# Fixing the issue order of the feed-forward stages of an encoder layer, with the second token chunk walked backwards

## The chip, the cores and the metric

One core of a Trainium2 chip runs the whole kernel. The time is device microseconds for one execution; the median of three runs of the kernel before is 1975.6 us (1968.54 to 1975.73). One further execution was profiled. It took 1982.1 us, of which the trace covers a span of 1980.3 us from the first to the last instruction.

## The reference

One layer of a bidirectional encoder on 1,536 tokens (1,024 of a prompt, 512 of a sample), all in float32, followed by a last RMSNorm:

```python
x = x + mix @ w_out                       # mix: two groups of attention heads, each normalised
hn = rms_norm(x, g_ffn)
x = x + (silu(hn @ w_gate) * (hn @ w_up)) @ w_down
y = rms_norm(x, g_final)
```

The model width is 1,024 and the hidden width (D_FF) 2,816. The change touches only the feed-forward part: gate and up products, the gated product, the down product, and the residual sum after it.

## The kernel before, in words

**Arithmetic.** Every float32 operand is split into a high part and a low part (hi on ScalarE as a copy, lo on VectorE as the difference), and a product is made of three matmuls per tile: hi x hi, hi x lo, lo x hi (mm3, L146). The feed-forward products use a Strassen-Winograd scheme: a 2 x 2 block product is done with seven products instead of eight, and sums of blocks are made before and after. So each operand exists in seven versions: some of the blocks themselves, the others sums or differences.

**Gate and up (gate_up, L1123).** The tokens are handled as two chunks of 768 (ck), the hidden units as 22 slices of 128 (f), so there are 44 steps u. A step makes the seven products in the order SEQ = 1, 6, 2, 7, 5, 4, 3. Each is four mm3 sets of 12 matmuls with 384 columns in a PSUM bank named x (mm), y or z. Between them stands the chain on the results: p1 copies product 1 on ScalarE, u2, u3, c22, c21, c12 are sums on VectorE (L1143 to L1160), sl1 and sl2 are Silu on ScalarE, and t1, t2 are the gated products on VectorE (L1157, L1164). Products 2, 7, 4, 3 accumulate into a bank that already holds another product, so each must wait until that one has been read: product 2 for p1, product 7 for u2, product 4 for u3, product 3 for c22. After every second slice GpSimd makes five sums of the results for the down products (L1175) and writes all seven versions to DRAM (hid_d, L1176). The results stand in a tile named as with two buffers, a12 and a21 with one each.

**Operands of a step.** w_sum (L1043) is a generator that prepares the seven weight versions of the next step, one portion after each product: GpSimd sums (fs, L1061), ScalarE hi (fhi, L1056), VectorE lo (flo, L1057). Its weights come through fw_load (L1031), 512 KB for gate and 512 KB for up, in three buffers named fraw, on the SP queue. h_sum (L983) makes the seven versions of a chunk: a sum where needed (mix, L991), hi (L1006) and lo (L1007), 1,536 columns each. raw_tile (L960) loads one of the six token tiles of a chunk, scales it on VectorE (L969, xh), transposes it with eight TensorE instructions (L210, pt) and copies the two results out on ScalarE and VectorE. The six tiles of chunk 1 are written in the main loop behind slices 5, 7, 9, 11, 13 and 15 (L1271).

**Down (L1314).** 42 products m of 33 matmuls with 512 columns: seven versions n in the order WSEQ = 2, 4, 3, 1, 6, 5, 7, each for six pairs of token tiles b (three of each chunk). The left operand comes back from hid_d (left, L1218, 704 KB, then hi and lo of 1,408 columns). The weights come as quarter tiles of 256 KB (wq, L1195), one or two for a piece, with a GpSimd sum where there are two (L1215), then hi and lo (dhi L1204, dlo L1205); eleven pieces make one version, and there is room for 22. x_back (L1280) reloads x for the residual. The buffers of this stage reuse the room of the gate and up stage, and a tile waits for the old tiles that it lies on.

**What sets the order.** The text gives every instruction its engine, and within one engine the framework's scheduler orders instructions by its own model of their times and their place in the text. So instructions of a later step can stand ahead of an earlier one's on a queue; matmuls of product 1 or 6 of slice u + 1 are found between those of slice u, and the left operands of the first down products were converted near 1330 us. SP's and GpSimd's DMA queues are ordered in the same way.

Of the kernel before, what the change touches and what calls it, by code (L numbers as in the profile page):

```python
# [8 lines left out]
F32 = mybir.dt.float32  # L9
# [47 lines left out]
def hymba_layer_kernel(  # L57
# [725 lines left out]
    def out_pre(i):  # L783
# [3 lines left out]
        o = room("qa", "o_in") if i < NO else late.tile([P, D], F32, tag="o_in", name="o_in", bufs=3)  # L787
# [172 lines left out]
    def raw_tile(ck, b, pool, tag, bufs, banks):  # L960
# [18 lines left out]
        transposed_whole(xh, put, banks)  # L979

    hpool, hsum = {}, {}

    def h_sum(n, eng=nc.gpsimd):  # L983

# [9 lines left out]
        if n == 1:  # L994
            src = b11
            if eng is nc.vector:
                mix(b12, b22, b12, ALU.subtract)
# [22 lines left out]
    steps = [(ck, f) for ck in range(2) for f in range(NFF)]  # L1020
    turn = dict(fs=0, fhi=0, flo=0)
# [9 lines left out]
    def fw_load(u, old=False):  # L1031
        if u < len(steps):
# [10 lines left out]
    def w_sum(u):  # L1043

        if u >= len(steps):
            while True:
                yield
# [3 lines left out]
        def temp():  # L1051
            return turned("fs", F32, 2, 2)
# [16 lines left out]
        parts(6, s2)  # L1069
        yield  # L1070
        parts(2, a12)
        if u == 0:
            yield
            g, up = wraw.pop(u)
            a11, a12, a21, a22 = g[:, :4], g[:, 4:], up[:, :4], up[:, 4:]
        s3 = temp()
        add(s3, a11, a21, ALU.subtract)
        if u > 0:
            yield
        parts(7, s3)  # L1080
        s4 = temp()
        add(s4, a12, s2, ALU.subtract)
        yield
        parts(5, s1)
        yield
        parts(4, a22)
# [34 lines left out]
    sums, a12, a21 = {}, {}, {}  # L1121

    def gate_up(u, extra=None):  # L1123
        ck, f = steps[u]
        j, odd = divmod(f, 2)
        if not odd:
            sums[ck, j] = fp.tile([P, 7, HC], F32, tag="as", name="as", bufs=2)
# [6 lines left out]
        for n in SEQ:  # L1134
            acc = {1: x, 2: x, 6: y, 7: y, 4: y, 5: z, 3: z}[n]
            (wh, wl), (hh, hl) = wsum.pop((u, n)), hsum[n]
# [28 lines left out]
            next(nxt)  # L1165
            if extra:
                extra(n)
        if not odd:
            a21[0] = t2
            return  # L1170

        A11, A12, A21, A22 = part[3], t1, a21[0], part[4]
        for n, p, q, op in ((5, A11, A12, ALU.add), (6, A21, A11, ALU.subtract), (2, A21, A22, ALU.add),
                            (1, A11, A22, ALU.add), (7, A12, A22, ALU.subtract)):
            nc.gpsimd.tensor_tensor(out=part[n], in0=p, in1=q, op=op)  # L1175
        nc.gpsimd.dma_start(out=hid_d[ck][:, :, j], in_=a.rearrange("p n (c t) -> p (n c) t", t=P))  # L1176
# [7 lines left out]
    down = [(n, b) for n in WSEQ for b in range(NB)]  # L1184
    PA, PB = 9, 13
    made = dict(piece=0, left=0)
# [20 lines left out]

    def piece(n, j):
        p, *q = quads(n, j)
        src = dpool["b"].tile([P, 512], F32, tag="wq", name="wq", bufs=6)  # L1210
# [223 lines left out]
```

## Time and profile before

| | |
|---|---|
| median of 3 runs | 1975.6 us |
| profiled execution | 1982.1 us |
| its span | 1980.3 us |
| TensorE (PE) busy | 1847.2 us, 93% |
| weight loads (PEld) busy | 1543.9 us, 78% |
| VectorE (DVE) busy | 1345.5 us, 68% |
| ScalarE (ACT) busy | 915.8 us, 46% |
| GpSimd (POOL) busy | 850.3 us, 43% |
| granted TensorE clock, mean | 0.962 |

A busy engine is one with an instruction running; matmuls overlap, so TensorE's share says only when it had something to do. The times between its instructions, and what ended them, tell more. In windows of the trace each column gives busy time and the number of instructions of an engine, then the granted TensorE clock as a part of full speed, the busy share of the 16 DMA engines and their rate.

### The profile page before, as it was taken

What the parts mean: (1) busy time and instruction counts of PE and PEld (TensorE: products, weight loads), DVE (VectorE), ACT (ScalarE), POOL (GpSimd) and SP (SyncE); (2) the same over time, 40 slices, a digit from 0 to 9 for tenths busy, and PEclk for the clock granted to TensorE, in tenths of its full rate; (3) what the DMA queues carried; (4) which work ended last, traced back from release to release, by engine and by line L of the source; (5) the groups of instructions that cost most, each with busy time, mean ns of one, the idle gap of its engine ahead of it and who ended that gap; (6) DMA issues with size and microseconds to landing.
All of it is one profiled execution on the core that took longest, in us unless ns stands there. A gap on an engine that the chain in (4) does not pass through costs nothing.

```text
span 1980.3 us, 27660 instructions
## 1 busy us (share of the span) xinstructions
PE 1847.2 (93%) x9682; PEld 1543.9 (78%) x9682; DVE 1345.5 (68%) x2554; ACT 915.8 (46%) x1667; POOL 850.3 (43%) x688
## 2 busy tenths in 40 slices
PE   6999999999899998799899999979999997999998
PEld 4666666667566666588899999979999995887886
DVE  7566756757656667565977677877767765756765
ACT  5465666656565566343433343433433332324431
POOL 3323333344355442100666566666567543642110
PEclk9999999999999898899999999989999998999999
DMA  7799899997898799443353343433443448866652
GB/s 261 139 178 165 169 180 157 179 153 148 162 166 171 160 218 191 157 154 113 107 147 124 110 124 103 120 100 105 118 131 103 133 126 323 271 219 215 222 174 94
DMA packets 421692, 316.26 MB, mean 160 GB/s; under 512 B 262336, under 2 KB 365904, under 8 KB 421552
## 3 DMA queue, kind: packets, MB, share of 16 engines
q1 hardware_dynamic: 398928, 229.93, 48.2%
q0 software_dynamic: 22624, 84.56, 15.3%
q8 instruction: 76, 1.25, 0.3%
q14 instruction: 64, 0.52, 0.1%
HBM read 202.71 MB, written 51.41 MB: 128 GB/s over the span
## 4 chain that ended last, share of the span: by engine, by line
PE 72%; DMA 13%; DVE 7%; issue 3%; ACT 2%; POOL 2%; SPq 1%; DVEq 0%; ACTq 0%; POOLq 0%
PE acc L155 36%; PE yacc L155 11%; PE mmacc L155 7%; PE zacc L155 7%; DMA pT<-p 6%; PE sc L687 4%; PE pv L755 3%; PE sc L686 2%; DVE flo L1057 2%; DMA left<-hid_d 1%; DMA hid_d<-as 1%; DMA vna<-va 1%; DMA wq<-in_w_down_dram 1%; DMA fraw<-in_w_up_dram 1%; PE pt L210 1%
## 5 line engine op out<-in xcount | busy, mean ns | idle before, releaser
L155 PE MATMUL acc<-dhi,left 128*128 128x512 f32 x924 | 291.2, 396 | 16.4 <-ACT left L1231 13.1
L155 PE MATMUL acc<-hth,whi 128*128 128x512 f32 x576 | 243.6, 423 | 1.6 <-ACT hth L285 1.5
L155 PE MATMUL acc<-htl,whi 128*128 128x512 f32 x576 | 240.9, 418 | 2.9 <-DVE htl L288 2.7
L155 PE MATMUL acc<-hth,wlo 128*128 128x512 f32 x576 | 240.5, 418 | 0.0
L1057 DVE TENSOR_TENSOR flo<-fs,fhi 128x512 fp32r<-128x512 f32 x176 | 173.3, 987 | 86.7 <-ACT fhi L1056 83.5
L155 PEld LDWEIGHTS acc<-dhi,left 128*128 128x128 f32 x924 | 175.0, 190 | 57.6 <-ACT left L1231 13.9
L1056 ACT ACTIVATE fhi<-fs 128x512 fp32r<-128x512 f32 x176 | 109.3, 628 | 190.1 <-POOL fs L1061 78.5
L125 POOL TENSOR_TENSOR wlo<-wraw,whi 128x1024 fp32r<-128x1024 f32 x48 | 117.8, 2456 | 182.7 <-ACT whi L124 158.9
L740 DVE SCALAR_TENSOR_TENSOR p<-t,p 128x768 f16<-128x768 f32 (+3 forms) x192 | 145.5, 765 | 72.4 <-ACT p L736 71.6
L734 ACT ACTIVATE t<-t,mt 128x768 f32<-128x768 f32 (+3 forms) x192 | 137.5, 716 | 122.2 <-DVE mt L727 119.6
L155 PE MATMUL acc<-dlo,left 128*128 128x512 f32 x462 | 182.3, 395 | 0.0
L1061 POOL TENSOR_TENSOR fs<-fraw 128x512 f32<-128x512 f32 x88 | 130.8, 1502 | 84.0 <-DMA fraw<-in_w_up_dram 74.8
L1057 DVE TENSOR_TENSOR flo<-fraw,fhi 128x512 fp32r<-128x512 f32 x132 | 165.7, 1255 | 1.3 <-ACT fhi L1056 1.3
L1215 POOL TENSOR_TENSOR wq<-wq 128x512 f32<-128x512 f32 x55 | 93.4, 1709 | 158.1 <-DMA wq<-in_w_down_dram 134.5
L736 ACT ACTIVATE p<-t 128x768 f16<-128x768 f32 (+3 forms) x192 | 118.1, 624 | 77.4 <-DMA pT<-p 48.7
L155 PEld LDWEIGHTS acc<-hth,whi 128*128 128x128 f32 x576 | 113.1, 196 | 35.2 <-issue 9.6
L155 PEld LDWEIGHTS acc<-htl,whi 128*128 128x128 f32 x576 | 113.0, 196 | 34.0 <-issue 6.5
L155 PEld LDWEIGHTS acc<-hth,wlo 128*128 128x128 f32 x576 | 113.1, 196 | 30.3 <-issue 6.8
L1056 ACT ACTIVATE fhi<-fraw 128x512 fp32r<-128x512 f32 x132 | 83.0, 629 | 116.3 <-PE yacc L155 93.5
L1232 DVE TENSOR_TENSOR left<-left,left 128x1408 fp32r<-128x1408 f32 x42 | 74.2, 1768 | 89.9 <-ACT left L1231 89.9
L755 PEld LDWEIGHTS <-pT 128*128 128x128 f16 x1536 | 72.7, 99 | 70.8 <-DMA pT<-p 38.1
L1175 POOL TENSOR_TENSOR as<-a,as 128x384 f32<-128x384 f32 x66 | 87.5, 1326 | 94.0 <-DVE a L1164 74.6
(210 smaller groups left out, 4755.8 us busy)
## 6 DMA issues: line engine op xcount, KB each, us to landing
wq<-in_w_down_dram SPq DMA_DIRECT2D x132, 256.0 KB
hid_d<-as POOLq DMA_DIRECT2D x22, 1344.0 KB, 8.0
left<-hid_d SPq DMA_DIRECT2D x42, 704.0 KB
wraw<-in_w_in_dram POOLq DMA_DIRECT2D x46, 512.0 KB, 5.9
fraw<-in_w_gate_dram SPq DMA_DIRECT2D x45, 512.0 KB
fraw<-in_w_up_dram SPq DMA_DIRECT2D x45, 512.0 KB
tabb<-in_tabb_dram POOLq DMA_DIRECT2D x8, 800.0 KB, 6.6
xh<-x_d SPq DMA_DIRECT2D x12, 512.0 KB
```

The costliest lines, as they stand in the source:

```text
L125: eng.tensor_tensor(out=lo, in0=src, in1=hi.bitcast(F32), op=ALU.subtract))
L155: latest[0] = nc.tensor.matmul(out=out, lhsT=a, rhs=b, start=first and i == 0, stop=i == last, skip_group_check=not first)
L687: nc.tensor.matmul(out=out, lhsT=qh[hs, qs], rhs=lx, start=False, stop=True)
L734: nc.scalar.activation(t, t, AF.Exp, bias=mt, scale=-1.0, accum_out=k.den)
L736: nc.scalar.activation(k.p16[:, 0], t, AF.Copy, scale=16384.0)
L740: nc.vector.scalar_tensor_tensor(out=k.p16[:, 1], in0=k.t, scalar=16384.0, in1=k.p16[:, 0], op0=ALU.mult, op1=ALU.subtract)
L755: nc.tensor.matmul(start=j + i == 0, stop=j + i == m, **one)
L1056: nc.scalar.activation(hi, src, AF.Copy)
L1057: nc.vector.tensor_tensor(out=lo, in0=src, in1=hi.bitcast(F32), op=ALU.subtract)
L1061: nc.gpsimd.tensor_tensor(out=o, in0=a, in1=b, op=op)
L1175: nc.gpsimd.tensor_tensor(out=part[n], in0=p, in1=q, op=op)
L1215: nc.gpsimd.tensor_tensor(out=src, in0=src, in1=other, op=q[1])
```

## The change

- From the opening of the feed-forward stage to the end of the kernel, all five engines (TensorE, ScalarE, VectorE, GpSimd and SP, the DMA queues with them) issue their instructions in the order of the text. What the text has ahead of it is ordered as before.
- Chunk 1 takes its slices from 21 down to 0. Slice 22 (the first of chunk 1) therefore uses the weights that slice 21 has just used; they are neither loaded nor split again.
- The five GpSimd sums after a pair of slices, and their write, are put in a list (todo) and issued one after each product of the next slice.
- The opening makes the chunk sums 7, 5, 4, 3 inside slice 0, on VectorE. The first step's weights aren't loaded a second time but for a quarter of up (256 KB). GpSimd's difference of two chunk blocks stands behind a chunk's last input tile.
- In the down stage, the first six products are versions 2 and 4 of chunk 0, the next six those of chunk 1. Loads of quarters and left operands are written ahead of their use (piece_load, left_load), the conversions later. x comes back one pair per place.
- Buffers: four fs in one pool instead of two in each of two, seven wq instead of six, two o_in instead of three.

```diff
-        o = room("qa", "o_in") if i < NO else late.tile([P, D], F32, tag="o_in", name="o_in", bufs=3)
+        o = room("qa", "o_in") if i < NO else late.tile([P, D], F32, tag="o_in", name="o_in", bufs=2)
...
         transposed_whole(xh, put, banks)
+        if b == CT - 1:
+            nc.gpsimd.tensor_tensor(out=raw[0, 1], in0=raw[1, 1], in1=raw[0, 1], op=ALU.subtract)
...
-    steps = [(ck, f) for ck in range(2) for f in range(NFF)]
+    steps = [(0, f) for f in range(NFF)] + [(1, f) for f in reversed(range(NFF))]
...
-        if u < len(steps):
+        if u < len(steps) and u != NFF:
...
-        if u >= len(steps):
+        if u >= len(steps) or u == NFF:
             while True:
                 yield
...
         parts(6, s2)
+        s3 = temp()
+        add(s3, a11, a21, ALU.subtract)
         yield
         parts(2, a12)
...
         s4 = temp()
         add(s4, a12, s2, ALU.subtract)
         yield
+        parts(7, s3)
+        yield
         parts(5, s1)
         yield
-        parts(4, a22)
+        parts(4, wraw.pop(-1) if u == 0 else a22)
         parts(3, s4)
...
-            (wh, wl), (hh, hl) = wsum.pop((u, n)), hsum[n]
+            (wh, wl), (hh, hl) = wsum[u - (u == NFF), n], hsum[n]
...
-            next(nxt)
             if extra:
                 extra(n)
+            next(nxt)
+            if todo:
+                todo.pop(0)()
...
+        def add(n, p, q, op):
+            todo.append(lambda: nc.gpsimd.tensor_tensor(out=part[n], in0=p, in1=q, op=op))
...
-    down = [(n, b) for n in WSEQ for b in range(NB)]
+    down = [(n, b) for ck in range(2) for n in WSEQ[:2] for b in range(ck * HT, ck * HT + HT)]
+    down += [(n, b) for n in WSEQ[2:] for b in range(NB)]
...
     def ahead(n):
 
         if n == 1:
-            left(0)
-            left(1)
+            left_load(0)
+            left_load(1)
...
+            left(0)
         elif n in (7, 5):
             for j in ((2, 3) if n == 7 else (4, 5)):
                 piece_parts(2, j, early[j])
+        elif n == 4:
+            left(1)
...
+    mine = {mybir.EngineType.Activation, mybir.EngineType.DVE, mybir.EngineType.PE, mybir.EngineType.Pool,
+            mybir.EngineType.SP}
+    ctx.enter_context(tc.manual_schedule(engines=mine))
+    t = fB[0].tile([P, NK, P], F32, tag="fraw", name="fraw", bufs=3)
+    wraw[-1] = t[:, 4:]
+    nc.sync.dma_start(out=wraw[-1], in_=w_up[4 * P:, :P].rearrange("(k p) f -> p k f", p=P))
     fw_load(1)
+    def opening_sums(n):
+
+        m = {1: 7, 6: 5, 2: 4, 7: 3}.get(n)
+        if m:
+            h_sum(m, nc.vector)
+            if m != 4:
+                next(first)
+
     for u, (ck, f) in enumerate(steps):
         extra = None
-        if f == NFF - 1:
-            extra = ahead if ck else h_sum
...
+        if u == 0:
+            extra = opening_sums
+        elif u == NFF - 1:
+            extra = lambda n: h_sum(n, nc.vector)
+        elif u == len(steps) - 1:
+            extra = ahead
+            fA.release()
         gate_up(u, extra)
         if ck == 0 and f >= 5 and f % 2 and f // 2 - 2 < CT:
             raw_tile(1, f // 2 - 2, fp, "xh", 1, "dn")
...
+    while todo:
+        todo.pop(0)()
+    for j in range(6, NP):
+        piece_load(2, j)
+    left_load(2)
+    x_back(0)
+    left_load(3)
     for j in range(6, NP):
         piece(2, j)
-    x_back(0)
-    left(2)
-    for b in range(1, NB):
-        x_back(b)
-    left(3)
+    x_back(1)
...
+    slices = {}
+    todo += [(4, j) for j in range(NP)]
+    for m in range(3):
+        slices[m] = [todo.pop(0) for _ in range((4, 4, 3)[m])]
+    for w in range(2, len(WSEQ)):
+        first, n = (6 * w - 3, 3) if w == 2 else (6 * w - 6, 6)
+        for b in range(n):
+            slices[first + b] = [(WSEQ[w], j) for j in range(NP * b // n, NP * (b + 1) // n)]
+    for p in slices[0][:3]:
+        piece_load(*p)
...
         if m:
-            left(m + 3)
...
+            left_load(m + 3)
+        if m == 0:
+            x_back(2)
+        elif m in (3, 4, 5):
+            x_back(m)
+        for p in slices.get(m, ()):
+            if p not in quarter:
+                piece_load(*p)
+        left(m + 2)
+        for p in slices.get(m, ()):
+            piece(*p)
+        for p in slices.get(m + 1, ())[:2]:
+            piece_load(*p)
```

## Rows read from the trace of the kernel before

**Rows 1.** Windows by stage: busy time and instructions of each engine, clock, DMA share, rate.
```profile
0.00:934.00 934.00, 854.08 (x4555) 617.25 (x4556) 605.83 (x1559) 531.29 (x1043) 316.88 (x321) 0.95 0.82 170
934.00:1636.00 702.00, 673.81 (x3762) 667.75 (x3761) 519.52 (x654) 270.97 (x464) 434.34 (x308) 0.97 0.40 118
1636.00:1972.00 336.00, 319.27 (x1369) 258.91 (x1367) 216.45 (x328) 112.84 (x158) 99.09 (x59) 0.97 0.63 220
```

**Rows 2.** Windows without a stop: gate and up stage, down stage.
```profile
1345.00:1620.00 275.00, 274.99 (x1573) 274.66 (x1572) 195.32 (x261) 104.59 (x185) 176.09 (x131) 1.00 0.41 119
...
1800.00:1960.00 160.00, 160.00 (x699) 131.04 (x698) 112.22 (x211) 58.88 (x90) 24.83 (x15) 1.00 0.55 189
```

**Rows 3.** Windows over the places where TensorE stops.
```profile
936.20:962.00 25.80, 18.35 (x85) 17.08 (x84) 24.70 (x29) 15.94 (x22) 12.59 (x7) 0.87 0.37 119
...
1089.00:1104.00 15.00, 11.09 (x52) 10.77 (x50) 11.63 (x11) 3.78 (x8) 10.01 (x6) 0.77 0.39 110
1273.00:1306.00 33.00, 23.21 (x92) 21.75 (x91) 32.57 (x23) 13.22 (x18) 25.54 (x12) 0.74 0.26 74
1329.00:1345.00 16.00, 9.35 (x41) 9.02 (x40) 9.46 (x13) 6.53 (x10) 4.98 (x4) 0.79 0.38 126
1636.00:1676.00 40.00, 26.85 (x105) 20.70 (x104) 18.52 (x20) 10.76 (x14) 10.80 (x7) 0.83 0.88 331
1776.00:1794.00 18.00, 14.77 (x55) 11.03 (x54) 9.86 (x12) 6.79 (x9) 2.10 (x1) 0.91 0.35 137
```

**Rows 4.** Windows of one stop and of the matmuls behind it.
```profile
1287.90:1292.00 4.10, 0.17 (x1) 0.00 (x0) 4.10 (x4) 0.63 (x1) 4.10 (x3) 0.88 0.00 0
1292.00:1296.10 4.10, 4.02 (x13) 4.02 (x14) 4.10 (x3) 0.03 (x1) 4.10 (x2) 0.50 0.02 4
```

**Rows 5.** Instructions by line: ns shortest/median/longest, first and last start, shape.
```profile
L1160 DVE TENSOR_TENSOR c<-zacc,u x44: 543/546/558, 968.6 to 1636.2; 128x384 f32<-128x384 f32 x44
...
L1162 ACT ACTIVATE sl<-c x44: 508/526/528, 969.2 to 1636.9; 128x384 f32<-128x384 f32 x44
...
L1164 DVE TENSOR_TENSOR as<-c,sl x22: 541/543/1645, 985.5 to 1637.4; 128x384 f32<-128x384 f32 x22
...
L1057 DVE TENSOR_TENSOR flo<-fs,fhi x176: 673/693/2094, 825.1 to 1619.8; 128x512 fp32r<-128x512 f32 x176
L1057 DVE TENSOR_TENSOR flo<-fraw,fhi x132: 674/1251/6778, 821.1 to 1616.6; 128x512 fp32r<-128x512 f32 x132
...
L969 DVE SCALAR_TENSOR_TENSOR xh<-xh,rs,g_f x12: 1272/1284/2322, 832.8 to 1080.6; 128x1024 f32<-128x1024 f32 x12
```

**Rows 6.** Instructions by line: the chunk sums, lo, hi and mix.
```profile
L1007 DVE TENSOR_TENSOR h4l<-q,h4h x2: 1746/1750/1753, 939.6 to 1303.7; 128x1536 fp32r<-128x1536 f32 x2
...
L1006 ACT ACTIVATE h4h<-q x2: 1466/1466/1467, 937.8 to 1296.6; 128x1536 fp32r<-128x1536 f32 x2
...
L991 DVE TENSOR_TENSOR q<-q,q x4: 1752/1754/1759, 900.6 to 941.3; 128x1536 f32<-128x1536 f32 x4
```

**Rows 7.** Instructions by line on GpSimd: chunk difference, weight sums, result sums.
```profile
L1267 POOL TENSOR_TENSOR q<-q,q x1: 3647/3647/3647, 1088.5 to 1088.5; 128x1536 f32<-128x1536 f32 x1
...
L1061 POOL TENSOR_TENSOR fs<-fs,fraw x44: 1254/1450/2807, 823.1 to 1605.4; 128x512 f32<-128x512 f32 x44
...
L1175 POOL TENSOR_TENSOR as<-a,as x66: 1002/1398/1993, 973.1 to 1640.9; 128x384 f32<-128x384 f32 x66
```

**Rows 8.** The chain of waits from 1326 to 1346 us: start, us, what.
```profile
1329.33 4.33 DMA left<-hid_d
```

**Rows 9.** The chain of waits from 1640 to 1680 us.
```profile
1642.77 7.73 DMA hid_d<-as
...
1651.01 4.39 DMA x<-x_d
...
1655.42 10.68 DMA left<-hid_d
```

**Rows 10.** Window with the highest DMA rate in the down stage.
```profile
1660.00:1670.00 10.00, 2.00 (x4) 1.19 (x5) 1.62 (x1) 1.38 (x1) 2.31 (x1) 0.50 1.03 406
```

**Rows 11.** The chain of waits from 1770 to 1800 us.
```profile
1779.42 6.02 DMA left<-hid_d
```

More of the change, by code (lines that the diff above doesn't have):

```diff
@@ L1119, in half @@
         return fp.tile([P, HC], F32, tag=tag, name=tag, bufs=bufs)
-    sums, a12, a21 = {}, {}, {}
+    sums, a12, a21, todo = {}, {}, {}, []
     def gate_up(u, extra=None):
@@ L1125, in gate_up @@
         j, odd = divmod(f, 2)
-        if not odd:
+        if (ck, j) not in sums:
             sums[ck, j] = fp.tile([P, 7, HC], F32, tag="as", name="as", bufs=2)
@@ L1164, in gate_up @@
                 v.tensor_tensor(out=t2, in0=c22, in1=sl2, op=ALU.mult)
-            next(nxt)
             if extra:
                 extra(n)
-        if not odd:
-            a21[0] = t2
-            return
[L1172 to L1176, printed above, removed]
+            next(nxt)
+            if todo:
+                todo.pop(0)()
+        if odd:
+            a12[ck, j] = t1
+        else:
+            a21[ck, j] = t2
+        if not ((ck, j) in a12 and (ck, j) in a21):
+            return
+        A11, A12, A21, A22 = part[3], a12[ck, j], a21[ck, j], part[4]
+        def add(n, p, q, op):
+            todo.append(lambda: nc.gpsimd.tensor_tensor(out=part[n], in0=p, in1=q, op=op))
+        add(5, A11, A12, ALU.add)
+        add(6, A21, A11, ALU.subtract)
+        add(2, A21, A22, ALU.add)
+        add(1, A11, A22, ALU.add)
+        add(7, A12, A22, ALU.subtract)
+        todo.append(lambda: nc.gpsimd.dma_start(out=hid_d[ck][:, :, j], in_=a.rearrange("p n (c t) -> p (n c) t", t=P)))
     NB = 2 * HT
     WSEQ = (2, 4, 3, 1, 6, 5, 7)
-    down = [(n, b) for n in WSEQ for b in range(NB)]
+    down = [(n, b) for ck in range(2) for n in WSEQ[:2] for b in range(ck * HT, ck * HT + HT)]
+    down += [(n, b) for n in WSEQ[2:] for b in range(NB)]
     PA, PB = 9, 13
-    made = dict(piece=0, left=0)
+    made = dict(piece=0)
     pieces, lefts, dpool = {}, {}, {}
@@ L1222, in left @@
         ck, c = divmod(b, HT)
[L1223 to L1224 removed]
+        slot = m % 4
         if slot < 2:
@@ L1227, in left @@
         else:
-            hi, lo = (dpool["b"].tile([P, NP, P], F32R, tag=f"left{i}", name=f"left{i}", bufs=2) for i in range(2))
-        raw_lo = lo.bitcast(F32)
-        nc.sync.dma_start(out=raw_lo, in_=hid_d[ck][:, (n - 1) * HT + c])
-        nc.scalar.activation(hi, raw_lo, AF.Copy)
-        nc.vector.tensor_tensor(out=lo, in0=raw_lo, in1=hi.bitcast(F32), op=ALU.subtract)
-        lefts[n, b] = (hi, lo)
+            hi, lo = (dl.tile([P, NP, P], F32R, tag=f"left{i}", name=f"left{i}", bufs=2) for i in range(2))
+        nc.sync.dma_start(out=lo.bitcast(F32), in_=hid_d[ck][:, (n - 1) * HT + c])
+        lefts[m] = (hi, lo)
+    def left(m):
+        if m < len(down):
+            hi, lo = lefts[m]
+            nc.scalar.activation(hi, lo.bitcast(F32), AF.Copy)
+            nc.vector.tensor_tensor(out=lo, in0=lo.bitcast(F32), in1=hi.bitcast(F32), op=ALU.subtract)
     early = []
```

52 lines of the change are left out of this document (14 added, 38 removed).

## The prediction

> **What bounds the kernel now.** I read the windows by stage first: the attention and output part up to 934 us, the gate and up products to 1636 us, the down products to 1972 us [rows 1]. The change touches the last two, and there TensorE is nearly always busy, so the question is what keeps it waiting. A quiet stretch gives the pace [rows 2]: 1573 matmuls in 275 us are 0.1748 us each, so a product of 12 takes 2.1 us and a slice of 84 takes 14.7 us. In the down stage 699 in 160 us are 0.2289 us each, 7.55 us for a product of 33. Next I laid windows over every place where TensorE stops [rows 3] and took from each the matmuls in it at that pace. Lost are: at the opening 25.8 - 85 x 0.1748 = 11 us; round 1089 us 6; at the change of chunk 17; round 1329 us 9; at the start of the down products 40 - 105 x 0.2289 = 16; round 1776 us 5. That is 64 us in all, and no order of the queues can win more than this. Part of it is no idle time: after the stop of 4.1 us the granted clock was 0.50, the 1.2 GHz level, and 13 matmuls took 4.1 us instead of 2.3 [rows 4]. A stop of four microseconds costs six.
>
> **What the change does to each place.** All five queues now run in the order of the text. An instruction that waits holds up everything written behind it on its engine. I go through the places where that order puts a late instruction ahead of an urgent one. Slices are counted 0 to 43, times from the first matmul of the slice.
>
> *The six input tiles of chunk 1, which the diff does not touch.* After slices 5, 7, ... 15, raw_tile scales a tile on VectorE and TensorE transposes it. Now these transposes stand between the third product of that slice and the first of the next. VectorE reaches the scaling only after what the slice's last product releases. In order that is c12, then sl2 on ScalarE, t2, the two splits 4 and 3 for the next slice, and the scaling itself. By the medians of [rows 5] this is 0.55 + 0.53 + 0.54 + 1.25 + 0.69 + 1.28 = 4.8 us, by the minima 4.2; contention with GpSimd may make it 5.5. TensorE has nothing else to do in that time, and then runs slowly, 4.1 - 13 x 0.1748 = 1.8 us by [rows 4]. So 6 x 6.6 = **40 us added** (36 to 46). Before, these transposes lay between matmuls of other groups: the last tile was scaled at 1080.6 us [rows 5], and of the six stretches only the opening holds any. The DMA of the tile is not what is late: it is issued in mid-slice, behind a weight load.
>
> *Opening.* Slice 0 now makes the chunk sums 7, 5, 4, 3, the rest of its own weight sums and those of slice 1. VectorE's queue up to u3 holds lo7, flo7, flo1, u2, mix5, lo5, flo5, mix4, lo4, flo6: five of 1.75 us [rows 6], four splits of about 1 us and one of 0.55, 13.3 us. It starts at 4.1 us (2.1 for the matmuls, 0.5 for p1 as for sl2, 1.5 for h7h) and waits 1.5 us twice for ScalarE after a mix. So u3 is done near 20.9, lo3 and flo4 near 23.6, and product 4 starts there instead of at 10.5. With the slow clock the slice loses about 14.5 us against 11 before: **+3.5** (-3 to +8). The smaller reload (256 KB instead of 1 MB) is worth nothing while VectorE is last; without that cover it is worth at most the 11 us.
>
> *Round 1089 us.* GpSimd's 3.65 us subtraction of the chunk's operands [rows 7] ran here, and a VectorE split beside it took 6.78 us, the maximum in [rows 5]. It moves behind the last input tile, where no PSUM result waits at first. I keep 1 of the 6 us: **-5** (-6 to 0). The Trainium skill ("SBUF — State Buffer", section "Who interferes with whom") says that VectorE instructions with two SBUF inputs and GpSimd instructions reading SBUF take turns on one port for their full length; the trace agrees here. What that would make of the rest is a rival below.
>
> *Change of chunk.* Slice 22 reuses the weights of slice 21: two loads, 7 splits on ScalarE and VectorE and 4 sums go. In slice 21 VectorE has, up to c12, six lo and three mixes of 1.75 us and six results of 0.55, 19.1 us, and waits three times 1.5 us behind a mix. From 4.1 us on that ends at 27.7. Behind it on ScalarE stand sl2, h3h (1.47) and only then p1 of slice 22, done at 30.2. Product 2 of slice 22, due at 14.7 + 4.2 = 18.9, waits 11.3 us, with the slow clock 13: **-4** against 17 (-9 to +2).
>
> *Round 1329 us.* The left operand of the first down product was converted 300 us early; ScalarE stood waiting 4.33 us for its DMA, with p1 and the PSUM chain behind it [rows 8]. Now it is loaded ahead and converted in slice 43. There u3 stands behind it, a stop of about 1.5 us: **-7.5** (-9 to -4).
>
> *Start of the down products.* Before, an x load on SP waited for the 7.73 us write of the last sums, and the left operand behind it landed late, after 10.68 us [rows 9]. Now the first six products read chunk 0 alone, and the last write is covered by 45 us of them. What is late next: pieces 9 and 10 lie on the room of a21 and a12 (dlo starts 14 + 22 + 48 + 26 = 110 KB into its pool, a12 at 110.5 KB), which GpSimd's last additions read. These end four times 1.4 us after t2 [rows 7], about 8 us after slice 43; piece 9 is due at 6.2 us. With the conversions TensorE stands about 3 us. Then all eleven pieces of sum 4 are wanted by the fourth product, not the seventh. Up to there SP asks for 5 + 22 quarters (7.1 MB), four left operands (2.9), six x tiles (3.1) and the gains (0.5), 13.6 MB. At the most that the trace shows, 406 GB/s with the DMA engines full [rows 10], that is 33.6 us; with the last sum and split (1.4 + 0.6 + 1.25) 36.9. There are 34.6: three products, 6.9 us of the fourth, the stop of 3, and 2 us in which loads start early. So it is 2 us late at that rate and 10 at the 331 GB/s of the stretch before [rows 3]. I take 5 us and the slow clock, with the first stop 10 in all against 16: **-6** (-12 to +6). The third set of pieces has again only three products, for 7.9 MB with fewer others: **+3** (0 to 8).
>
> *Round 1776 us.* Left operands landed late there, one after 6.02 us [rows 11], with quarters ahead of them on SP. Loads now precede the pieces of each product: **-5** (-5 to 0).
>
> *Between these places.* After the last product of a slice VectorE owes t2 and three splits before u2. By the chain above that is 1.6 + 1.25 + 0.69 + 1.25 + 0.55 = 5.3 us, due at 6.3. The cover is 1 us. In the 21 slices with additions on GpSimd it may be gone by 0.2 us: **+4** (0 to 12). The product groups, o_in with two buffers and the write order change nothing that TensorE waits for.
>
> **Sum.** 40 + 3.5 - 5 - 4 - 7.5 - 6 + 3 - 5 + 4 = +23 us. The profiled execution took 1982.1 us (span 1980.3), 6.5 us above the median of 1975.6. From 1982.1 it gives 2005, at the median's level 1998. A measurement here can tell about 0.5% (10 us) from no change.
>
> **Rivals.**
> *The tiles cost nothing; faster.* If VectorE came to the scaling before the slice's last product ended, the 40 us fall away: 1998 - 40 = 1958. It decides as soon as the scaling stands ahead of c12 in VectorE's queue. For it: all other places together give -17. Against it: raw_tile is called after gate_up, and the PSUM chain is written inside. Chance 0.15.
> *A draw.* The order binds less than I think on some engine, or the two crowded slices do better: opening -3, chunk -9, down start -12, no stops between, tiles 37. That sums to 37 - 3 - 5 - 9 - 7.5 - 12 + 0 - 5 + 0 = -5, between 1971 and 1985. Or the change does not hold TensorE to the text; then groups of slice u + 1 still appear within slice u and the time stays near 1976. Chance 0.15.
> *The port shared by VectorE and GpSimd.* In a slice with additions GpSimd needs at least 4 x 1.25 + 5 x 1.0 us [rows 7] and VectorE 7 x 0.67 + 2 x 0.54 [rows 5]. If they always took turns, that is 15.8 us against 14.7. With a fixed order 1.1 us could be lost 21 times, 23 us instead of 4: 2017. This is the rule of the skill's page named above, carried through. Against it: over 275 us with the same work TensorE was always busy [rows 2], as the following slice has room. Chance 0.12.
>
> **How the numbers follow.** The forecast itself has 0.58, and 1980 to 2015 as its own range. With the port rival, slower has 0.70; same 0.15; faster 0.15. The range of 1964 to 2028 takes in the draw, the port rival and the upper bounds of tiles and down start; it leaves out the faster rival and a rest above.
>
> **What would show it.** Right: after each of slices 5, 7, ... 15 a stop of 4 to 6 us before pt on TensorE, released by xh on VectorE, and a slow clock behind it; one long stop at product 4 of slice 0 and one at product 2 of slice 22; none at 1329 us; in the down stage a short stop in the first product and one at the fourth. Wrong: no wait of pt for xh, or stops of over half a microsecond in most slices. If the tiles cost 40 us and the sum still fails, the two crowded slices or the DMA term were mis-sized.

## The result and the profile after

The kernel after takes 2047.8 us in the median of 4 runs (2041.8 to 2052.4), the kernel before 1974.7 us beside it; the ratio is 1.0375, with a 95% interval of 1.0338 to 1.0412. The profiled execution took 2045.0 us. So the change makes the kernel slower, as forecast, but by 63 us from profile to profile where +23 stood, and outside the range. (From median to median it is 73 us: the profiled execution of before lay 7 us above its median, that of after 3 us below. What follows explains the 63.)

The windows by stage answer to [rows 1]. Columns are as there.

```profile
0.00:932.00 932.00, 853.25 (x4552) 616.42 (x4553) 606.73 (x1557) 532.24 (x1043) 322.92 (x324) 0.95 0.83 170
932.00:1697.00 765.00, 683.69 (x3746) 672.50 (x3745) 516.22 (x651) 247.24 (x457) 424.51 (x297) 0.95 0.35 104
1697.00:2035.00 338.00, 325.74 (x1388) 262.91 (x1386) 205.88 (x329) 112.30 (x158) 87.46 (x62) 0.97 0.65 225
```

The loss is in the second row. To compare it with before I take the gate and up stage from the last output-projection matmul to the first down matmul. Before, the two stages overlap: 936.0 to the last gate or up matmul at 1636.2 is 700.2 us; less 20 down matmuls inside it (4.6) and plus 12 of product 6 ahead of it (2.1) this is 698 us. After, it is 765.1: **67 us more**. The down stage gave back some.

TensorE's waits, costliest first, name the two causes: six waits of the tiles' transposes for xh, and 17 short ones of product 7 for u2 (columns: who waited, for whom, us in total, times, longest).

```profile
PE pt L210 <- DVE xh L969: 42.4, 6, 7.6
...
PE yacc L155 <- DVE u L1137: 21.8, 17, 2.0
...
PE mmacc L155 <- ACT p L1134: 6.4, 1, 6.4
PE acc L155 <- ACT left L1245: 5.5, 1, 5.5
```

The third wait, for p1, came to 9.8 us in four places before. Before, no product waited for u2 in this stage (three waits of product 4 for u3 came to 11.0 us), and no transpose of these tiles waited. The windows over the single places answer to [rows 3]: the opening, the old place of the 1089 us stop, the change of chunk, the start of the down products, and round 1776 us.

```profile
932.00:961.00 29.00, 20.58 (x87) 18.43 (x86) 21.87 (x31) 13.81 (x18) 8.15 (x6) 0.76 0.17 54
1333.00:1369.00 36.00, 26.40 (x130) 25.44 (x129) 27.23 (x24) 12.94 (x15) 15.19 (x10) 0.86 0.09 26
...
1697.00:1745.00 48.00, 35.88 (x134) 26.32 (x133) 24.61 (x28) 15.75 (x22) 24.51 (x18) 0.86 0.95 347
1776.00:1794.00 18.00, 18.00 (x80) 14.65 (x79) 7.57 (x9) 4.02 (x5) 5.14 (x4) 1.00 0.70 230
1089.00:1104.00 15.00, 15.00 (x85) 15.00 (x85) 6.53 (x11) 3.87 (x8) 2.67 (x3) 0.97 0.44 128
```

At the pace of [rows 2] the first loses 29.0 - 87 x 0.1748 = 13.8 us (14.5 forecast), the second 13.3 (13 forecast), the third 48.0 - 134 x 0.2289 = 17.3 (10 forecast), the last two nothing. The last two show the same times as before, not the same work, but the old stops are not elsewhere either: the 6.4 us at the change of chunk are the only wait for p1, and the last wait of the down products ends at 1743.4 us. So the crowded slices were sized right as a whole. What was not is seen in VectorE's timeline at the first tile stop (start, us, instruction, the idle time before it and what ended it), where product 3 has just ended and TensorE stands until 1045.4:

```profile
1037.88 0.56 DVE L1154 TENSOR_TENSOR c<-zacc,u 128x384 f32<-128x384 f32 x1 [0.36 <-PE zacc L155]
1039.09 0.94 DVE L1158 TENSOR_TENSOR as<-c,sl 128x384 f32<-128x384 f32 x1 [0.65 <-ACT sl L1156]
1039.95 1.75 DVE L1056 TENSOR_TENSOR flo<-fraw,fhi 128x512 fp32r<-128x512 f32 x1
1041.62 1.48 DVE L1056 TENSOR_TENSOR flo<-fs,fhi 128x512 fp32r<-128x512 f32 x1
1043.02 2.28 DVE L969 SCALAR_TENSOR_TENSOR xh<-xh,rs,g_f 128x1024 f32<-128x1024 f32 x1
```

The instructions and their order are the ones forecast: c12, the wait for sl2, t2, two splits, the scaling. But the scaling takes 2.28 us, close to the maximum in [rows 5] (2.32), not its median of 1.28; the splits 1.75 and 1.48 us. At the sixth tile the same chain looks like this:

```profile
1240.02 0.56 DVE L1154 TENSOR_TENSOR c<-zacc,u 128x384 f32<-128x384 f32 x1 [0.33 <-PE zacc L155]
1241.23 0.56 DVE L1158 TENSOR_TENSOR as<-c,sl 128x384 f32<-128x384 f32 x1 [0.65 <-ACT sl L1156]
1241.75 0.69 DVE L1056 TENSOR_TENSOR flo<-fraw,fhi 128x512 fp32r<-128x512 f32 x1
1242.36 0.68 DVE L1056 TENSOR_TENSOR flo<-fs,fhi 128x512 fp32r<-128x512 f32 x1
1242.96 1.28 DVE L969 SCALAR_TENSOR_TENSOR xh<-xh,rs,g_f 128x1024 f32<-128x1024 f32 x1
```

It is 3 us shorter. What differs is GpSimd. In the window of the first stop it is busy for all of 7.50 us (fifth pair of numbers), in that of the sixth, the last one, for none:

```profile
1037.90:1045.40 7.50, 0.00 (x0) 0.00 (x0) 6.75 (x5) 1.56 (x3) 7.50 (x6) 0.78 0.24 70
1045.40:1052.40 7.00, 6.96 (x34) 6.99 (x35) 1.39 (x3) 1.61 (x3) 5.28 (x5) 0.74 0.12 34
...
1244.30:1250.30 6.00, 5.91 (x22) 5.95 (x23) 0.69 (x1) 0.64 (x2) 3.10 (x1) 0.50 0.22 67
1240.00:1244.40 4.40, 0.01 (x1) 0.04 (x1) 3.57 (x5) 1.56 (x3) 0.00 (x0) 0.90 0.13 38
```

These are the additions that it makes in the first stop:

```profile
1038.61 1.00 POOL L1174 TENSOR_TENSOR as<-as,a 128x384 f32<-128x384 f32 x1
1039.56 1.58 POOL L1060 TENSOR_TENSOR fs<-fs,fraw 128x512 f32<-128x512 f32 x1
1041.11 1.44 POOL L1174 TENSOR_TENSOR as<-a,as 128x384 f32<-128x384 f32 x1
1042.51 1.71 POOL L1060 TENSOR_TENSOR fs<-fraw 128x512 f32<-128x512 f32 x1
1044.18 1.97 POOL L1174 TENSOR_TENSOR as<-a,as 128x384 f32<-128x384 f32 x1
```

Read with VectorE's lines above, they show the two engines taking turns. The addition of 1039.56 ends at 1041.14, and the split of 1039.95 ends 0.56 us later, at 1041.70. The addition of 1041.11 ends at 1042.55, the split of 1041.62 at 1043.10, again 0.55 us later. The next addition ends at 1044.22, and the scaling at 1045.30. A split takes 0.68 us alone, so nearly all of it runs after the addition has ended; what the trace gives as its length is mostly the wait. So each of VectorE's instructions here waits out one of GpSimd's: against the sixth tile that is 0.38 + 1.06 + 0.80 + 1.00 = 3.2 us, the whole of the difference.

GpSimd's timeline in a slice with result sums (here at 1385 us, where product 7 waits for u2) shows what it does: sums of weights (L1060) and of results (L1174) one behind the other without a break, from before the slice's end until after u2.

```profile
1387.08 1.01 POOL L1174 TENSOR_TENSOR as<-as,a 128x384 f32<-128x384 f32 x1
1388.05 1.61 POOL L1060 TENSOR_TENSOR fs<-fs,fraw 128x512 f32<-128x512 f32 x1
1389.62 1.47 POOL L1174 TENSOR_TENSOR as<-a,as 128x384 f32<-128x384 f32 x1
1391.04 1.73 POOL L1060 TENSOR_TENSOR fs<-fraw 128x512 f32<-128x512 f32 x1
1392.73 1.46 POOL L1174 TENSOR_TENSOR as<-a,as 128x384 f32<-128x384 f32 x1
```

VectorE's four instructions in front of u2 there take 0.97, 1.78, 1.49 and 1.77 us. In the next slice, without result sums, the three splits take 0.68 each and u2 is in time.

### The profile page after: what moved, and what is told of

The parts are those of the page before. It is cut to its first block, busy times and chain, and to the rows that moved or that the text cites. A ratio compares the mean times of both kernels' runs of the same rounds, so it can differ in the third digit from the quotient of the medians.

```text
span 2043.3 us, 27575 instructions
## 1 busy us (share of the span) xinstructions
PE 1862.7 (91%) x9682; PEld 1551.8 (76%) x9682; DVE 1332.7 (65%) x2549; ACT 892.5 (44%) x1660; POOL 834.9 (41%) x682
## 3 DMA queue, kind: packets, MB, share of 16 engines
q8 instruction: 76, 1.25, 0.3%
## 4 chain that ended last, share of the span: by engine, by line
PE 68%; DVE 9%; DMA 8%; issue 3%; ACT 2%; POOL 1%; SPq 1%; DVEq 0%; ACTq 0%; POOLq 0%
PE acc L155 33%; PE yacc L155 12%; PE zacc L155 8%; PE mmacc L155 6%; DMA pT<-p 6%; DVE flo L1056 4%; PE sc L687 3%; PE pv L755 3%; PE sc L686 2%; DMA wq<-in_w_down_dram 1%; PE pt L210 1%; DMA vna<-va 1%; DVE c L1154 1%; DVE xh L969 1%; ACT sl L1156 1%
## 5 line engine op out<-in xcount | busy, mean ns | idle before, releaser
L1060 POOL TENSOR_TENSOR fs<-fraw 128x512 f32<-128x512 f32 x85 | 129.8, 1527 | 236.3 <-DMA fraw<-in_w_up_dram 150.7
L1056 DVE TENSOR_TENSOR flo<-fs,fhi 128x512 fp32r<-128x512 f32 x172 | 160.8, 935 | 50.1 <-ACT fhi L1055 50.1
L1226 POOL TENSOR_TENSOR wq<-wq 128x512 f32<-128x512 f32 x55 | 78.3, 1426 | 200.8 <-DMA wq<-in_w_down_dram 200.2
L1156 ACT ACTIVATE sl<-c 128x384 f32<-128x384 f32 x44 | 23.1, 525 | 289.4 <-DVE c L1154 289.4
L1056 DVE TENSOR_TENSOR flo<-fraw,fhi 128x512 fp32r<-128x512 f32 x129 | 130.9, 1015 | 24.3 <-ACT fhi L1055 24.3
L1055 ACT ACTIVATE fhi<-fs 128x512 fp32r<-128x512 f32 x172 | 104.6, 621 | 26.5 <-PE yacc L155 23.8
L687 PE MATMUL sc<-kb,qa 64*128 64x512 f32 (+2 forms) x256 | 114.4, 449 | 0.0
L686 PE MATMUL sc<-ka,qa 128*128 128x512 f32 (+2 forms) x256 | 100.7, 395 | 8.4 <-DVE mt L727 8.3
```

The source lines that it names most:

```text
L686: nc.tensor.matmul(out=out, lhsT=qh[:, qs], rhs=kx, start=True, stop=False)
L687: nc.tensor.matmul(out=out, lhsT=qh[hs, qs], rhs=lx, start=False, stop=True)
L1055: nc.scalar.activation(hi, src, AF.Copy)
L1056: nc.vector.tensor_tensor(out=lo, in0=src, in1=hi.bitcast(F32), op=ALU.subtract)
L1060: nc.gpsimd.tensor_tensor(out=o, in0=a, in1=b, op=op)
L1226: nc.gpsimd.tensor_tensor(out=src, in0=src, in1=other[0], op=quads(n, j)[2])
```

## The experiments

**Theory A**: the excess comes from GpSimd's run of additions, which the fixed order puts beside VectorE's chain at the slice's end. The rivals stand in the expectations. All kernels are edits of the one after. The part ahead of the change, the same in all, took between 924 and 952 us in the profiled executions, so kernels are compared by the length of the gate and up stage, as above. Each length comes from one execution; the down stage, whose text is the same in all, took 337 to 342 us, so differences under some 5 us may be scatter. A whole time without a ratio is one run. The medians of the kernel before, run beside them, were 1982.1 us for 1 to 4, 1983.9 for 5 to 8 and 1981.0 for 9 to 11.

| kernel | edit | stage, us | whole, us | ratio to before (95%) |
|---|---|---|---|---|
| before | | 698 | | |
| after | | 765.1 | 2047.8 | 1.0375 (1.0338 to 1.0412) |
| 1 | zeros written, no result sums | 737.8 | 2020.1 | |
| 2 | result sums on VectorE | 754.7 | 2050.5 | |
| 3 | tiles early | 707.2 | 2010.8 | |
| 4 | 2 and 3 | 715.5 | 1994.1 | 1.0069 (1.0038 to 1.0099) |
| 5 | result sums on GpSimd, in mid-slice | 740.9 | 2024.8 | |
| 6 | 5 and 3 | 701.5 | 1985.3 | 1.0001 (0.9970 to 1.0032) |
| 7 | 3, sums on VectorE behind u2 | 748.8 | 2032.0 | |
| 8 | chunk 1 forward | 772.2 | 2061.6 | |
| 9 | t2 behind the next u2 | 745.0 | 2031.3 | |
| 10 | 6 and 9 | 688.6 | 1969.6 | 0.9946 (0.9912 to 0.9981) |
| 11 | 10, chunk sums in order of need | 685.2 | 1967.0 | 0.9923 (0.9895 to 0.9951) |

**1. No result sums.** The five sums are left out; GpSimd writes zeros in their place.

```diff
-            todo.append(lambda: nc.gpsimd.tensor_tensor(out=part[n], in0=p, in1=q, op=op))
+            todo.append(lambda: nc.gpsimd.memset(part[n], 0.0))
```

> The five sums that GpSimd makes after a pair of slices are left out: it writes zeros in their place, an instruction that reads nothing from SBUF. Everything else, and the order, stays. Theory A (VectorE's instructions with two SBUF inputs are held up by GpSimd's run of ten such instructions, which the new order puts beside the chain at the slice's end): the splits in that chain fall from 1.5-1.8 us to about 0.7, the 17 stops before product 7 (u2, 1.3 us each) go, five tile stops fall from 7.6 us to between 4.4 and 6.5; 2045 becomes about 2012 (2003 to 2022). Theory B (the order of VectorE's queue alone makes these stops, whatever GpSimd does): the stops stay at 1.3 and 7.6 us, the time within 8 us of 2045.

Stage -27 us, and the whole, 2020.1 us, is inside theory A's range. The waits:

```profile
PE pt L210 <- DVE xh L969: 36.8, 6, 6.5
...
PE yacc L155 <- DVE u L1137: 1.6, 2, 1.4
```

All u2 stops but two are gone, without anything taken off VectorE. The tile stops keep 6.5 us, since the sums of weights still stand beside the splits; with GpSimd idle the sixth has 4.4.

**2. The sums on VectorE**, at the same places.

```diff
-            todo.append(lambda: nc.gpsimd.tensor_tensor(out=part[n], in0=p, in1=q, op=op))
+            todo.append(lambda: nc.vector.tensor_tensor(out=part[n], in0=p, in1=q, op=op))
```

> The same five sums are made on VectorE, at the same places of the text; nothing is left out. Theory A: GpSimd's run is gone, so the splits at the slice's end take about 0.7 us and the stops before product 7 go, although VectorE has 0.55 us more ahead of u2; tile stops 4.4 to 6.5 us; about 2015 (2003 to 2025). Theory B: VectorE's queue ahead of u2 and of the tiles only gets longer: stops of 1.3 + 0.6 us and more, about 2060 (2050 to 2075).

Theory A's time was missed: the stage gains 10 us, and 17 stops by u2 stay, 21.2 us. The whole, 2050.5, falls into theory B's range, but the part ahead took 15 us more here than in the kernel after, and the stops did not grow as theory B had it. VectorE's timeline shows why they stay:

```profile
1391.51 1.37 DVE L1158 TENSOR_TENSOR a<-c,sl 128x384 f32<-128x384 f32 x1 [0.65 <-ACT sl L1156]
1392.81 1.78 DVE L1056 TENSOR_TENSOR flo<-fraw,fhi 128x512 fp32r<-128x512 f32 x1
1394.51 0.68 DVE L1056 TENSOR_TENSOR flo<-fs,fhi 128x512 fp32r<-128x512 f32 x1
1395.12 0.68 DVE L1056 TENSOR_TENSOR flo<-fraw,fhi 128x512 fp32r<-128x512 f32 x1
1395.72 1.63 DVE L1174 TENSOR_TENSOR as<-as,a 128x384 f32<-128x384 f32 x1
1397.27 0.54 DVE L1137 TENSOR_TENSOR u<-yacc,p 128x384 f32<-128x384 f32 x1
```

Two splits are short now, but the first result sum stands in front of u2 and takes 1.63 us beside a sum of weights, where the later ones take 0.54.

**3. Tiles early.** The tile is loaded one slice earlier and scaled behind product 7 instead of at the slice's end; the transposes stay where they are.

```diff
+        elif ck == 0 and f >= 5 and f % 2 and f // 2 - 2 < CT:
+            extra = lambda n, b=f // 2 - 2: tile_scale(1, b) if n == 7 else None
         gate_up(u, extra)
+        if ck == 0 and f >= 4 and f % 2 == 0 and f // 2 - 2 < CT:
+            tile_load(1, f // 2 - 2, fp, "xh", 1)
```

> GpSimd's sums as in the changed kernel. Only the six input tiles of chunk 1: their load is written one slice earlier, and the scaling on VectorE stands behind u3 in the middle of slices 5, 7, ... 15; the transposes stay where they are. Both theories: no wait of the transposes for the scaling, 42 us of idle time and some 15 us of slow clock go, less about 1 us for each scaling in mid-slice: 2045 becomes about 1992 (1983 to 2003). Rival (the tile's DMA or the PSUM banks hold the transposes up too): stops of over 3 us stay there and the gain is under 25 us. The stops before product 7 stay at 1.3 us.

Stage -58 us, no transpose waits, and the 17 stops by u2 stay (21.1 us). The whole, 2010.8, is over the range expected, since the part ahead took 20 us more here than in the kernel after. The 58 us are the whole price of the six tiles in this order: 42.4 us of waits and some 15 behind them, most of it at a lower clock (0.74 over the 7 us behind the first stop, in the windows above).

**4. The edits of 2 and 3 together.**

> The sums on VectorE and the scaling in mid-slice together; nothing is left out. Theory A: the two gains add, about 57 + 25 us less VectorE's added work of some 3 us: about 1966 (1955 to 1982), a little under the kernel before. Theory B: only the tiles' part is won, and the sums make u2 later: about 2005 (1995 to 2020).

1.0069 of before: most of the loss is back, but 23 stops by u2 are left (28.9 us), more than with 3 alone, since the first sum still stands in front of u2 as in 2. The time of 1994.1 us misses both forecasts, theory A's 1966 and, just, theory B's 2005.

**5. The sums on GpSimd in mid-slice**, in the order 5, 7, 6, 2, 1. This tells the place of GpSimd's work from its amount.

```diff
-            if todo:
+            for _ in range(min(len(todo), {7: 2, 5: 3, 4: 1}.get(n, 0))):
                 todo.pop(0)()
```

> The five sums stay on GpSimd, but in mid-slice: two behind product 7, three behind product 5, the write behind product 4. The amount of work on every engine is that of the changed kernel. Theory A (it matters that GpSimd's run stands beside VectorE's chain at the end of the slice): VectorE has the port to itself from the last product to u2, so at most 3 of the 17 stops that u2 ends (21.8 us) stay, the tile stops fall from 7.6 to about 6.3 us, and the gate and up stage goes from 765 to about 738 us (732 to 744), the whole to about 2018. Rival (the amount of GpSimd's work counts, not its place): the stops only move to other products, those ended by u3, c22 or the splits, and the stage gains under 8 us.

Stage -24 us with no work removed, almost as much as in 1. The rival falls.

```profile
PE pt L210 <- DVE xh L969: 35.4, 6, 6.2
...
PE yacc L155 <- DVE u L1137: 5.0, 8, 1.4
```

Eight stops stay and not three, five of them of 0.2 us: the sums of weights now come later and still meet two of the splits.

**6. The edits of 5 and 3 together.**

> Both causes taken away at once: the sums on GpSimd in mid-slice, and the six input tiles of chunk 1 loaded a slice earlier and scaled in mid-slice, behind product 7. Theory A: no wait of pt for xh, few stops by u2, the gate and up stage takes about 681 us (674 to 692) against about 698 of the kernel before, and the whole is 0.99 of the kernel before (0.983 to 0.998). Rival (the scaling and the sums now meet in the same mid-slice stretch and hold up u3 or c22 there): stops of over a microsecond ended by u3 or c22 in most of the slices with sums, the stage over 695 us and the ratio 1.0 or above.

No transpose waits, and the kernel is level with before, but the stage takes 701.5 us and not 681; 11.4 us of u2 stops in 18 places stay, and the two crowded slices lose about what they lost. Time and ratio are those of the rival, but not its reason: product 4 waits for u3 in two places only (4.3 us). The gains of 3 and 5 do not add, since 7 of the 24 us in 5 were shorter tile stops, which 3 takes away anyway, and u2 has more stops left than in 5 (11.4 us against 5.0).

**7. Sums on VectorE, behind u2**, in the order 5, 7, 6, 2, 1, on top of 3.

```diff
-            if todo:
+            if todo and n != 1:
                 todo.pop(0)()
...
-            todo.append(lambda: nc.gpsimd.tensor_tensor(out=part[n], in0=p, in1=q, op=op))
+            todo.append(lambda: nc.vector.tensor_tensor(out=part[n], in0=p, in1=q, op=op))
```

> Tiles early as before, and the five sums on VectorE, but none ahead of u2: they are issued behind products 6, 2, 7, 5 and 4. If the stops that stayed with the sums on VectorE came from the one sum in front of u2, and not from VectorE's load as such, the stops by u2 fall from 23 to at most 4 and the stage takes about 685 us (678 to 695). If VectorE's load as such is the limit, stops by u3, c22 or later u2 take their place and the stage stays above 700.

28 stops by u2, 45.9 us. The stage stays above 700 us, as the second account had it, but neither account was right. VectorE is not full: even in the slice with sums it waits 0.48 and 0.46 us for TensorE in front of c22 and c21. The timelines of VectorE and GpSimd at the end of a slice with sums point to another cause:

```profile
1408.63 2.42 DVE L1170 TENSOR_TENSOR as<-c,sl 128x384 f32<-128x384 f32 x1 [0.65 <-ACT sl L1168]
1410.98 1.77 DVE L1068 TENSOR_TENSOR flo<-fraw,fhi 128x512 fp32r<-128x512 f32 x1
1412.68 1.77 DVE L1068 TENSOR_TENSOR flo<-fs,fhi 128x512 fp32r<-128x512 f32 x1
```

```profile
1407.92 1.38 POOL L1193 DMA_DIRECT2D hid_d<-as  x1 [8.60 <-DVE as L1186]
1409.17 1.46 POOL L1072 TENSOR_TENSOR fs<-fraw 128x512 f32<-128x512 f32 x1
1410.71 1.49 POOL L1072 TENSOR_TENSOR fs<-fs,fraw 128x512 f32<-128x512 f32 x1
1412.16 1.73 POOL L1072 TENSOR_TENSOR fs<-fraw 128x512 f32<-128x512 f32 x1
```

The write of the results is still on GpSimd's queue. It waited there 8.60 us for VectorE's last sum, and the sums of weights behind it were pushed exactly beside t2 and the splits. So sums of weights do the same harm as sums of results; it matters what GpSimd does while VectorE owes something. t2 fares worst: it begins 0.54 us before the addition of 1409.17, while GpSimd still issues the write, and yet ends 0.42 us after it. That the place of the write is the cause is read from the timelines; no run moves the write alone.

**8. Chunk 1 forward**, weights of its first slice loaded and split again.

```diff
-    steps = [(0, f) for f in range(NFF)] + [(1, f) for f in reversed(range(NFF))]
+    steps = [(0, f) for f in range(NFF)] + [(1, f) for f in range(NFF)]
```

> The changed kernel with chunk 1 walked forward and the weights of its first slice loaded and split again. If the backward walk saves what the prediction said, two loads, seven splits on each of ScalarE and VectorE and four sums, in the one slice where VectorE is far behind, the stop at the change of chunk is longer by 6 to 10 us and the stage takes about 774 us (768 to 785) instead of 765. Rival (the splits find room in slice 21 or do not lie on the path): within 3 us of 765.

Stage +7.1 us, inside the expected range; the wait of product 2 for p1 at the change of chunk went from 6.4 to 10.9 us, 4.5 more and not the 6 to 10 expected. Part of the rest is u2 stops, 25.4 us instead of 21.8. So the backward walk pays at its own place: slices 20 to 23 take 81.3 us together without it and 76.2 with it.

**9. t2 late**, with everything else as in the kernel after.

```diff
                 v.tensor_tensor(out=u2, in0=y, in1=p1, op=ALU.add)
+                while owed:
+                    owed.pop()()
...
-                v.tensor_tensor(out=t2, in0=c22, in1=sl2, op=ALU.mult)
+                owed.append(lambda: v.tensor_tensor(out=t2, in0=c22, in1=sl2, op=ALU.mult))
```

> Only t2 is moved: it is written behind u2 of the next slice instead of behind Silu at the end of its own. All sums and tiles stay where the change puts them, so GpSimd's run still stands beside the splits. Theory A (what u2 and xh wait for is VectorE's chain in front of them): the chain loses t2, 0.94 to 2.4 us beside GpSimd, and the wait of 0.65 us for Silu. At most 6 of the 17 u2 stops stay, under 6 us of 21.8, the tile stops go from 7.6 to about 6 us, and the gate and up stage from 765 to about 739 us (731 to 747). Rival (GpSimd's run holds VectorE for its whole length, whatever stands in the chain): the run just overlaps other instructions, u2 keeps over 10 of its stops and the stage stays above 752.

Stage -20 us, inside the expected range; u2 stops are 6.7 us in ten places, where at most six were expected. So an urgent result behind work that nobody waits for is the second half of the cause, and either half can be taken away. The tile stops stayed at 7.3 us, against the expectation; the timeline has the reason:

```profile
1039.61 0.56 DVE L1156 TENSOR_TENSOR c<-zacc,u 128x384 f32<-128x384 f32 x1 [0.37 <-PE zacc L155]
1041.34 1.77 DVE L1056 TENSOR_TENSOR flo<-fraw,fhi 128x512 fp32r<-128x512 f32 x1 [1.17 <-ACT fhi L1055]
1043.03 1.48 DVE L1056 TENSOR_TENSOR flo<-fs,fhi 128x512 fp32r<-128x512 f32 x1
1044.43 2.28 DVE L969 SCALAR_TENSOR_TENSOR xh<-xh,rs,g_f 128x1024 f32<-128x1024 f32 x1
```

The split's high part stands behind sl2 on ScalarE. VectorE now waits for it in the 1.17 us in which it made t2 before, so taking t2 out of the chain to xh shortens the stop by 0.3 us only.

**10. The edits of 6 and 9 together.**

> The kernel with sums in mid-slice and tiles early, and t2 behind the next u2 as well. There 18 stops by u2 are left, 11.4 us: GpSimd's sums of weights, which start when the up weights land or when the write of the results has been issued, still stand beside t2 and the splits. Theory A: with t2 out of the chain they go to under 3 us, the stage takes about 690 us (685 to 696) instead of 701.5, the whole 0.994 of the kernel before (0.989 to 1.0). Rival (the stops came from the copies of the tiles' transposes on VectorE and from p1 on ScalarE): over 6 us of them stay and the stage is above 697.

Stage 688.6 us, 9.4 under before, and the whole 0.9946 of it. This was the forecast of theory A, although 9 stops by u2 (5.6 us) stay.

**11. 10, and the chunk sums in the order in which they fall due.** The mixes are made ahead of the conversions, and lo 5, 4 and 3 wait until slice 22.

```diff
+    CHANGE = {(0, 1): ((h_hi, 1), (h_lo, 1)),
+              (0, 6): ((h_mix, 6), (h_hi, 6)),
+              (0, 2): ((h_hi, 2),),
+              (0, 7): ((h_lo, 6), (h_hi, 7)),
+              (0, 5): ((h_lo, 2),),
+              (0, 4): ((h_lo, 7), (h_mix, 5)),
+              (0, 3): ((h_hi, 3),),
+              (1, 1): ((h_hi, 5),),
+              (1, 6): ((h_lo, 5), (h_mix, 4), (h_hi, 4)),
+              (1, 2): ((h_lo, 4),),
+              (1, 7): ((h_lo, 3),)}
```

> The same, with the chunk sums of the two crowded slices in the order in which they fall due: each mix is made an instruction or more ahead of its high part's use, so that VectorE need not wait 1.5 us for ScalarE behind it, u3 and c22 stand ahead of conversions that are due later, and p1 of slice 22 stands ahead of the conversion of product 5. Theory: the two crowded slices are bound by the order on VectorE, not by its work alone: the stop at product 2 of slice 22 (6.2 us) goes, that at product 4 of slice 21 (3.8) falls under 1.5, the opening loses 3 us less, and the stage takes about 680 us (672 to 688), the whole 0.989 (0.984 to 0.995). Rival (VectorE's work in those slices is the limit): the stops only move to slices 22 and 23, and the stage gains under 4 us on the kernel with three edits.

Only 3.4 us for the stage, within the range expected but as the rival had it. Slice 0 gives 2.9 of them, as expected. At the change of chunk the stop at product 2 of slice 22 falls from 6.1 to 3.1 us, but one of 5.0 now stands at product 4 of that slice: the work is only paid elsewhere. Still, this kernel is faster than before, at 0.9923 of it, as is 10; the step from 10 to 11 alone lies inside the intervals and the scatter.

## Why the prediction was wrong

The sign and nearly all places were right: six tile stops where they were named, for the reason named (the scaling behind what product 3 releases, shown by 3); the longest stop of the opening at product 4 of slice 0 and a stop at product 2 of slice 22; none left of those round 1089, 1329 and 1776 us; a u3 stop in slice 43 (0.9 us, 1.5 forecast). In the two crowded slices only the totals were right, and that is in part luck: the opening lost its time in six stops, the longest 3.0 us, and the 11.3 us forecast at product 2 of slice 22 were 6.4 there and 2.8 at product 4 of slice 21. The forecast failed mainly in two terms of its sum, and both by the same step: **VectorE's instructions at the slice's end were priced at their medians of before**, where each of them had to wait out one of GpSimd's additions.

- *Tiles, +40.* The chain was added up to 4.8 us, of which "contention with GpSimd may make it 5.5". The stop was 7.6 us five times, and 4.4 the one time that GpSimd was idle. With the slow clock behind it the whole is 58 us (3). One member of the sum hardly lay on the path: t2, beside which ScalarE makes the split's high part, of much the same length (9). The bound was wrong, too: the maxima in [rows 5] (1.65 for t2, 2.1 for a split of sums, 2.3 for the scaling) were there to be added.
- *Between the places, +4.* "The cover is 1 us" rested on the same medians, and the chain to u2 was over it in every second slice from 1385 us on: there t2 and the splits take 6.0 us and not 3.7, 2.3 more, which is the cover and a stop of 1.3 us. There are 21.8 us of u2 stops in all, 20.0 without the 1.8 that lie in the windows of the two crowded slices. The stage gains 27 us in 1 and 24 in 5, of which 6 and 7 are shorter tile stops. This is the size that the port rival had (23 us instead of 4), given a chance of 0.12. Its rule, that the two engines take turns, is what the traces show. Its reckoning, that a slice's work no longer fits into the slice, is not: with the same work in mid-slice (5) 5.0 us of u2 stops are left. What spoke against the rival was that TensorE was always busy over 275 us before [rows 2]. But that was the order of the scheduler, which may place GpSimd's run and the splits elsewhere in the slice; the change fixes just this order, so a quiet stretch of before was no evidence for after.
- *Down, -6 + 3 - 5.* The excess over the pace fell by 2.4 us, not 8. The start lost 17.3 us (16 before) and not 10: the quarters for the second piece set came late, as the upper value of the DMA term had it. GpSimd's sum waited for quarters, ScalarE's conversion of the pieces for the sum, and the left operand behind it on ScalarE's queue ended a stop of 5.5 us at 1728 us. The window gives 347 GB/s there, near the 331 of the upper bound.

The three misses are 58 - 40, 20.0 - 4 and -2.4 + 8, so 18, 16 and 6 us; together they make up the 40 us between +23 and +63. That the two causes are enough for the loss is shown by 6, which moves only these two and comes out level with before. What the fixed order can gain shows only in 10 and 11, where u2 no longer stands behind t2.

The median of a split of unsummed weights fell from 1.25 us before [rows 5] to 0.68 after:

```profile
L1056 DVE TENSOR_TENSOR flo<-fraw,fhi x129: 676/683/1789, 820.7 to 1683.1; 128x512 fp32r<-128x512 f32 x129
```

Of all splits in the stage 160 of 305 took over 0.8 us before and 97 of 298 after. So fewer of them run beside GpSimd than before, and still the stage is slower: the slow ones now stand where TensorE waits for the chain. A median can fall while the path gets longer.

## What to carry to other kernels

When an order is fixed by hand, price each chain that ends in a wait with the durations of what will run beside it, not with medians of the old order; where the old trace has a maximum under the same neighbour, use that. Here the price is simple: a VectorE instruction with both operands in SBUF that meets GpSimd's run of additions takes its own time and up to one addition (1.0 or 1.25 us) more. Put results that the next product waits for ahead of work that only a later stage needs (t2), scale or convert inputs a half slice before their use, and keep the other engine's run in the part of the slice where nothing is owed. A DMA issue that waits on a compute queue moves everything behind it, too.

## What the runs showed of the hardware

Beside GpSimd's additions, VectorE's instructions with two operands in SBUF took longer: a split mostly 1.5 to 1.8 us instead of 0.68, t2 0.94 to 1.7 instead of 0.56, the scaling 2.28 instead of 1.28. Those with one operand in PSUM (c12, u2) kept their 0.55. The Trainium skill ("SBUF — State Buffer", section "Who interferes with whom") says that a VectorE instruction with two SBUF inputs contends with a GpSimd instruction that reads SBUF and not with one that only writes it. The traces agree, with experiment 1 for the second half: with zeros written there, no u2 stop was left but two, and a split beside the zeros took 0.69 us (at 1410.90). The two engines took turns for whole instructions, as the prediction had put the rule: in the kernel after, all of the 124 slowed splits, t2 and scalings between 980 and 1630 us ended 0.4 to 1.1 us after one of GpSimd's additions, which is their own length alone less 0.1 to 0.2. The wait stands in the trace as length, on both engines: an addition of 1.0 us took 1.44 to 1.97 in the first tile stop. So a busy GpSimd or VectorE may be one that waits.

The turns are not always one for one. Where an addition stands behind the write's DMA issue on GpSimd's queue, a VectorE instruction that begins during the issue waits out both: t2 took 2.3 to 2.8 us in 20 slices of experiment 7, and the split of 6.78 us in [rows 5] stood beside such an issue and three additions in a row. What holds VectorE during the issue is not shown; where the next addition still waited for its weights, VectorE's t1 kept its 0.56 us beside an issue (3, at 1103.01).

A stop of 4.4 us was followed by 6 us at a granted clock of 0.50 (the 1.2 GHz level), in the window at 1244.3 above; 22 matmuls were done in it: eight short transposes, and 14 of the products, which take 14 x 0.1748 = 2.4 us at the quiet pace. So this stop cost more than half as much again behind it. Behind the first stop, of 7.6 us, the clock was 0.74 over 7 us, and 26 matmuls of the products (4.5 us at the quiet pace) and eight transposes were done: the longer stop did not cost more behind it.
